# Batch norm after a matmul: the last chunk of the first column group in column layout, the row sums taken during it, and later normalisations on VectorE

## The chip, the cores and the metric

The kernel runs on one core of a Trainium2 chip. The metric is the device time of one execution in microseconds (us). Five engines work side by side, each on its own queue, in the order in which its instructions stand: TensorE (PE in the profile), VectorE (DVE), ScalarE (ACT), GpSimd (POOL) and SyncE (SP, which here only issues transfers). Sixteen DMA engines move the data between the memory of the chip and the core.

## The reference

```python
def reference(x, weight, gamma, beta, eps):      # x (16, 512, 1024), weight (1024, 768), f32
    y = np.matmul(x, weight)
    mean = np.mean(y, axis=(0, 1), keepdims=True)
    var = np.var(y, axis=(0, 1), keepdims=True)
    y_norm = (y - mean) / np.sqrt(var + eps)
    return (gamma * y_norm + beta).astype(np.float32)
```

So 8192 rows by 1024 are multiplied with 1024 by 768, and each of the 768 columns is normalised over all 8192 rows. No output of a column can be stored before all rows of that column are multiplied.

## The kernel before

**Tiling.** The rows are cut into C = 16 chunks of 512 (`CH`), a chunk into RT = 4 row tiles of 128. The columns are cut into NT = 6 column tiles of 128. The first GA = 3 column tiles are the first group (384 columns, half of the output); column tiles 3, 4 and 5 come after it, one at a time. x and the weight are read as f32 and cast to bf16 by the transfers that load them. GpSimd issues these (`load_x`, `load_w`); x is turned on VectorE (`turn_x`), so that the contraction lies on the partitions.

**Two layouts in the first group.** The chunks in `COLS` (line 58) are multiplied with the columns on the partitions (`mm`, line 184): 512 rows lie along the free dimension, VectorE takes the statistics of each column with `bn_stats` (`bn`, L297), ScalarE keeps the product in bf16 (`keep`, L300). Such a product must be transposed back by TensorE before it can be stored. The other ten chunks are multiplied with the rows on the partitions (`mm_rows`, L178). They need no transposing, but a column's sum then runs over the partitions: ScalarE squares the tile (`square`, L200), VectorE adds it to `sum1` (`add_rows`, L207), GpSimd adds the square to `sum2` (`add_squares`, L204; every fourth goes to VectorE and `sum3`), ScalarE keeps the tile in bf16 (`keep_rows`, L213). `merge_rows` (L216) adds `sum3` to `sum2`. Twelve small matmuls on TensorE (`sums_rows`, L234) add `sum1` and `sum2` over the partitions into the PSUM tile `tot`.

**The affine of the first group.** `part_cols` (L218) aggregates the statistics of the column chunks while row chunks are still being multiplied. `affine_rows` (L239) joins both parts to mean and variance, and makes scale and shift (the square root is on ScalarE, L247). For the column chunks these are used as they are. For the row chunks they must lie along the free dimension on every partition: two diagonal matrices times a matrix of ones (`spread_rows`, L264) put them there, and ScalarE copies the shift to `sum1` (L266).

**The outputs.** A row chunk is multiplied by the scale on VectorE (`norm_rows`, L272), shifted on GpSimd (`shift_rows`, L278), and stored in two pieces of 384 KB (`store_rows`, L282). A column chunk, and each chunk of column tiles 3 to 5, is normalised in place in bf16 (`norm`: on ScalarE in L317, on VectorE or GpSimd in L322), transposed on TensorE (`turn_y`, L338), copied from PSUM to the ring buffer on ScalarE (`out_copy`, L351), and stored (`store`, L356). Transposes that wait are taken up one after each matmul of `mm` (`turn_one`); the rest are flushed ahead of the copy. Tiles 3 and 4 give 8 blocks of 512 KB each, of two chunks. The last tile has its own plan (`last_outputs`), with buffers of its own (`o_sb`), since all that is left after the last product is its normalising, transposing, copying and storing.

**The order.** Nothing is decided while the kernel runs. Each step is put down with a due time, `at(t, function, ...)`; all are sorted by due time, and in that order they are appended to the queues of their engines. `pe` is the planned time of TensorE, `S` is `pe` at the end of the first group's products. `tk` is the due time of the column chunks' outputs and `tr` that of the row chunks'. Each engine keeps to its order: an instruction that waits holds all that stands behind it. The due times order the work and no more; the chip's times are in the profile. Input pieces and output pieces share one ring buffer (`piece`), eight PSUM banks serve all products and transposes, and all stores are issued by SyncE in one order.

Of the kernel before, what the change touches and what calls it, by code (L numbers as in the profile page):

```python
# [10 lines left out]
def kernel(  # L11
# [23 lines left out]
    nc = tc.nc  # L35
    f32 = mybir.dt.float32
    bf16 = mybir.dt.bfloat16
    AF = mybir.ActivationFunctionType
    ALU = mybir.AluOpType
# [5 lines left out]
    P = 128  # L45
# [3 lines left out]
    RT = CH // P  # L49
    C = M // CH  # L50
# [4 lines left out]
    EARLY = 5  # L55
    SHORT = 2
    GA = 3
    COLS = (0, 3, 5, 8, 10, 13)
    NA = GA * P
    GY = 3  # L60

# [3 lines left out]
    singles = ctx.enter_context(tc.tile_pool(name="singles", bufs=1))  # L65
# [7 lines left out]
    def seq(bi):  # L73

        ins = bi.ins
        prev = last.get(ins.engine)
        if prev is not None:
            tc.add_manual_dep(
                ins, prev,
                mybir.DependencyInfo(mybir.DependencyClass.NoSync, mybir.DependencyReason.DATA),  # L80
                reason="order",
            )
        last[ins.engine] = ins.name
        return bi
# [14 lines left out]
    sum2 = singles.tile([P, NA], f32)  # L99
    sum3 = singles.tile([P, NA], f32)  # L100
    for acc in (sum1, sum2, sum3):
        seq(nc.vector.memset(acc, 0.0))
    stats = singles.tile([P, NT, C, 6], f32)
    part1 = singles.tile([P, GA], f32)
    part2 = singles.tile([P, GA], f32)
    mv = singles.tile([P, NT, 2], f32)
    gamma_sb = singles.tile([P, NT], f32)
    beta_sb = singles.tile([P, NT], f32)
# [2 lines left out]
    tmp = singles.tile([P, NT], f32)  # L111
# [7 lines left out]
    xs, xT, py, ygrp, yrow, ops, ost, aff = {}, {}, {}, {}, {}, {}, {}, {}  # L119
# [4 lines left out]
    def piece(words):  # L124
        if head[0] + words > RING:
            head[0] = 0
        head[0] += words
        return ring[:, head[0] - words:head[0]]
# [71 lines left out]
        seq(nc.scalar.activation(sq_sb, py["row", c, s][:, 0:NA], AF.Square))  # L200

    def add_squares(c, s):
        eng, acc = (nc.vector, sum3) if s == RT - 1 and c < C - 2 else (nc.gpsimd, sum2)
        seq(eng.tensor_add(acc, acc, py.pop(("sq", c, s))))  # L204

    def add_rows(c, s):
# [7 lines left out]

    def merge_rows():
        seq(nc.gpsimd.tensor_add(sum2, sum2, sum3))  # L216

    def part_cols():  # L218

        g, share = slice(0, GA), len(COLS) / C  # L220
        for nt in range(GA):
            seq(nc.vector.bn_aggr(mv[:, nt, :], stats[:, nt, 0:len(COLS), :]))
        seq(nc.vector.tensor_mul(part2, mv[:, g, 0], mv[:, g, 0]))
        seq(nc.vector.tensor_add(part2, part2, mv[:, g, 1]))
        seq(nc.vector.tensor_scalar(part2, part2, share, None, op0=ALU.mult))
        seq(nc.vector.tensor_scalar(part1, mv[:, g, 0], share, None, op0=ALU.mult))

    def sums_rows():

# [9 lines left out]
    def affine_rows():  # L239
        g = slice(0, GA)  # L240
        mean, var = mv[:, g, 0], mv[:, g, 1]
        seq(nc.vector.tensor_add(mean, aff["tot"][:, 0:GA], part1))
        seq(nc.vector.tensor_mul(tmp[:, g], mean, mean))
        seq(nc.vector.tensor_sub(tmp[:, g], part2, tmp[:, g]))
        seq(nc.vector.tensor_add(var, aff["tot"][:, GA:2 * GA], tmp[:, g]))
        seq(nc.vector.tensor_scalar(var, var, 0.0, None, op0=ALU.max))
        seq(nc.scalar.activation(std[:, g], var, AF.Sqrt, bias=eps_sb, scale=1.0))  # L247
        seq(nc.vector.tensor_mul(tmp[:, g], mean, gamma_sb[:, g]))
        seq(nc.vector.reciprocal(std[:, g], std[:, g]))
        seq(nc.vector.tensor_mul(scale[:, g], std[:, g], gamma_sb[:, g]))  # L250
        diag = piece(2 * NA).rearrange("p (i a n) -> p i a n", i=2, n=P)
        aff["diag"] = diag
        for a in range(GA):
            seq(nc.vector.tensor_scalar(diag[:, 0, a], ident, scale[:, a:a + 1], None, op0=ALU.mult))
        seq(nc.vector.tensor_mul(tmp[:, g], tmp[:, g], std[:, g]))
        seq(nc.vector.tensor_sub(shift[:, g], beta_sb[:, g], tmp[:, g]))
        for a in range(GA):
            seq(nc.vector.tensor_scalar(diag[:, 1, a], ident, shift[:, a:a + 1], None, op0=ALU.mult))
# [36 lines left out]
    def bn(nt, c):  # L295
        i = c if nt >= GA else COLS.index(c)
        seq(nc.vector.bn_stats(stats[:, nt, i, :], py[nt, c]))  # L297
# [67 lines left out]
    def at(t, fn, *args):  # L365
        events.append((t, len(events), fn, args))
# [31 lines left out]
    pe = 0.0  # L398

    def rows_unit(c, s, jws=range(JW), span=ROW_US):  # L400
        nonlocal pe
        pe = max(pe, arrive[c * RT + s])
        at(pe, mm_rows, c, s, jws)
        pe += span
        if jws[-1] == JW - 1:
            at(pe + 0.2, square, c, s)
            at(pe + 0.7, add_rows, c, s)
            at(pe + 0.9, add_squares, c, s)
            at(pe + 1.6, keep_rows, c, s)

    def unit(nt, c, span, jws=range(JW)):
        nonlocal pe
        pe = max(pe, arrive[c * RT + RT - 1])
        at(pe, mm, nt, c, jws)
        pe += span
        if jws[-1] == JW - 1:
            at(pe + 0.2, bn, nt, c)
            at(pe + 1.0, keep, nt, c)
# [12 lines left out]
    pe = max(pe, arrive["w", 2])  # L431
    for nt in range(NT):
        unit(nt, 0, MM_US / 2, [2, 3])
    for c in range(1, C):
        if c in COLS:
            for nt in range(GA):
                unit(nt, c, MM_US)
        else:
            for s in range(RT):
                rows_unit(c, s)  # L440
        if c < EARLY:
            for nt in range(GA, NT):
                unit(nt, c, MM_US)
        if c == C - 2:
            at(pe + 0.5, part_cols)
            at(pe + 3.0, merge_rows)

    S = pe
    at(S + 2.0, sums_rows)
    at(S + 2.1, affine_rows)  # L450
    at(S + 5.5, spread_rows, 0)
    at(S + 5.6, spread_rows, 1)
    ga = tuple(range(GA))
    tr, tk = S + 7.2, S + 8.0
    for c in range(C):
        if c in COLS:
            for nt in range(GA):
                at(tk - 2.6 + 0.8 * nt, norm, nt, c, "act")
            for s in range(0, RT, 2):
                at(tk + 0.7 * s, turn_y, ga, c * CH + s * P, 2)  # L460
                at(tk + 0.7 * s + 1.9, out_copy, ga, c * CH + s * P, "act")
                at(tk + 0.7 * s + 2.7, store, ga, c * CH + s * P, 2)
            tk += 6.2
        else:
            for s in range(0, RT, 2):
                at(tr, norm_rows, c, s)
                at(tr + 1.1, shift_rows, c, s)
                at(tr + 3.0, store_rows, c, s)
                tr += 1.85

    def outputs(nt, t0, step):
        for b in range(C // 2):
            tb = t0 + step * b
            for i in range(2):
                at(tb - 1.4 + 0.5 * i, norm, nt, 2 * b + i, "act" if i or b < 2 else "dve")
            at(tb, turn_y, (nt,), 2 * b * CH, 2 * RT)
            at(tb + 2.2, out_copy, (nt,), 2 * b * CH, "act")
            at(tb + 2.3, store, (nt,), 2 * b * CH, 2 * RT)
# [16 lines left out]
    for nt in range(GA, NT):  # L495
        for c in range(EARLY, C):
            for jws in halves:
                unit(nt, c, MM_US / 2 + (0.12 if nt == GA else 0.17), jws)
        at(pe + 0.55, finish, nt)
        if nt == GA:  # L500
            outputs(nt, S + 40.0, 2.2)
        elif nt < NT - 1:
            outputs(nt, max(pe + 4.0, S + 55.0), 2.0)
        else:
            last_outputs(nt, pe + 3.0)
# [39 lines left out]
```

## Time and profile before

| what | before |
|---|---|
| time, median of 3 | 229.54 us (229.26 to 229.68) |
| span of the profiled execution | 228.0 us |
| TensorE busy | 202.1 us, 89% |
| VectorE busy | 149.0 us, 65% |
| ScalarE busy | 128.5 us, 56% |
| GpSimd busy | 122.7 us, 54% |
| read / written | 36.71 MB / 25.17 MB |
| loads, share of the 16 DMA engines | 59.1% |
| stores, share of the 16 DMA engines | 35.5% |

The span has three stages. To about 103 us x arrives, and the first group and part of the other tiles are multiplied as it comes. From there to 138 us nothing is transferred; the first group is finished at 125.97 us (the first product of the last stretch of `mm` starts there), its affine is done at 133.5. From 138 us to the end outputs are stored, while TensorE works through column tiles 3, 4 and 5, whose last statistics start at 202.7 us. After that only the last tile's outputs are left.

In the profile's rows an arrow reads "output from input", "x28" is a count, and brackets hold the idle time of the engine before an instruction with what ended it. An engine's share of the whole span says little here, since the three stages have different limits; stretches of the last stage say more.

### The profile page before, as it was taken

The numbers are of one execution on the slowest core, as the hardware profiler recorded it, in microseconds if no ns is written. First come the engines' busy times: TensorE is split into PE (matmuls) and PEld (weight loads), VectorE is DVE, ScalarE is ACT, GpSimd is POOL, SyncE is SP. The second block draws the span as 40 slices with busy tenths as digits, with TensorE's granted clock in tenths as the row PEclk, the third lists the DMA queues.
The fourth block names the chain that finished last, engine by engine and source line by source line (L and its number), as shares of the span: only waits on it lengthen the run. The fifth ranks groups of instructions, "written<-read, shape, count | busy, mean of one in ns | idle before, by whom it ended". The sixth has DMA issues, their size and how long they took to land. (4 is left out here: it accounts for less than half of the span.)

```text
span 228.0 us, 3342 instructions
## 1 busy us (share of the span) xinstructions
PE 202.1 (89%) x1148; PEld 104.6 (46%) x1166; DVE 149.0 (65%) x245; ACT 128.5 (56%) x224; POOL 122.7 (54%) x145
## 2 busy tenths in 40 slices
PE   7759999999999999999999999998999999876600
PEld 2333545444544654556456544444445555445400
DVE  3222888887787797978546387799786544348810
ACT  2001554442543664536546358788899999998300
POOL 8787595964765896615328409997998000002000
PEclk9988999999999999999999999999999999997755
DMA  5999999999999999980000004889896998998996
GB/s 63 166 187 186 174 196 196 197 194 196 192 192 196 197 196 196 196 116 0 0 0 4 0 0 175 293 303 337 320 358 235 314 294 236 263 282 248 285 283 207
DMA packets 70049, 43.74 MB, mean 192 GB/s; under 512 B 3984, under 2 KB 69520, under 8 KB 70032
## 3 DMA queue, kind: packets, MB, share of 16 engines
q0 software_dynamic: 34624, 18.36, 59.1%
q1 hardware_dynamic: 35408, 25.18, 35.5%
q8 instruction: 9, 0.15, 0.3%
q14 instruction: 8, 0.07, 0.1%
HBM read 36.71 MB, written 25.17 MB: 271 GB/s over the span
## 5 line engine op out<-in xcount | busy, mean ns | idle before, releaser
L188 PE MATMUL y_ps<-xT_sb,w_sb 128*128 128x512 bf16 (+1 forms) x522 | 130.7, 385 | 4.6 <-DVE xT_sb L166 2.1
L188 PEld LDWEIGHTS <-w_sb 128*128 128x128 bf16 x540 | 51.9, 97 | 69.1 <-issue 7.0
L300 ACT CAST y_sb<-y_ps 128x512 bf16<-128x512 f32 x66 | 39.8, 604 | 55.6 <-DVE stats L297 52.6
L297 DVE BATCH_NORM_STATS2 stats<-y_ps 128x6 f32<-128x512 f32 x66 | 44.8, 687 | 31.7 <-PE y_ps L188 30.9
L154 POOL DMA_DIRECT2D ring<-in_x_dram x72 | 45.3, 634 | 17.9 <-DVE xT_sb L166 9.6
L178 PE MATMUL y_ps<-w_sb,xT_sb 128*128 128x384 bf16 x320 | 53.1, 326 | 0.0
L338 PE MATMUL o_ps<-ident,y_sb 128*128 128x128 bf16 x264 | 45.4, 233 | 8.2 <-ACT y_sb L317 3.7
L166 DVE STREAM_TRANSPOSE xT_sb<-ring 128x1024 f32<-128x1024 f32 (+1 forms) x34 | 39.4, 1168 | 15.7 <-DMA ring<-in_x_dram 15.4
L204 POOL TENSOR_TENSOR sum<-sum,sq_sb 128x384 f32<-128x384 f32 x32 | 32.2, 1005 | 24.5 <-ACT sq_sb L200 23.5
L278 POOL TENSOR_TENSOR ring<-ring,sum 128x768 f32<-128x768 f32 x20 | 36.2, 1836 | 11.4 <-ACT sum L266 8.2
L178 PEld LDWEIGHTS <-xT_sb 128*128 128x128 bf16 x320 | 31.3, 98 | 21.6
L317 ACT ACTIVATE y_sb<-y_sb,shift,scale 128x512 bf16<-128x512 bf16 x38 | 31.5, 859 | 0.0
L351 ACT CAST ring<-o_ps 128x1024 f32<-128x1024 bf16 (+1 forms) x28 | 27.0, 988 | 5.3 <-POOL ring L278 2.1
L338 PEld LDWEIGHTS <-y_sb 128*128 128x128 bf16 x264 | 23.2, 103 | 14.0 <-ACT y_sb L317 6.7
L207 DVE TENSOR_TENSOR sum<-y_ps,sum 128x384 f32<-128x384 f32 x40 | 21.8, 545 | 11.3 <-ACT sq_sb L200 10.5
L200 ACT ACTIVATE sq_sb<-y_ps 128x384 f32<-128x384 f32 x40 | 19.5, 493 | 11.2 <-PE y_ps L178 9.7
L213 ACT CAST y_sb<-y_ps 128x384 bf16<-128x384 f32 x40 | 19.1, 477 | 7.2 <-DVE sum L207 7.1
L272 DVE TENSOR_TENSOR ring<-y_sb,a_ps 128x768 f32<-128x768 bf16 x20 | 18.6, 939 | 1.7 <-DMA out_dram<-ring 1.7
L322 POOL TENSOR_SCALAR y_sb<-y_sb,scale,shift 128x512 bf16<-128x512 bf16 x2 | 1.7, 845 | 30.2 <-DVE shift L311 30.2
L322 DVE TENSOR_SCALAR y_sb<-y_sb,scale,shift 128x512 bf16<-128x512 bf16 x26 | 11.6, 478 | 0.0
L147 PE MATMUL idle_ps<-idle_sb 128*128 128x512 bf16 x26 | 7.7, 468 | 1.2 <-DVE idle_sb L92 1.2
L141 POOL DMA_DIRECT2D w_sb<-in_weight_dram x12 | 6.1, 511 | 0.7 <-DMA ring<-in_x_dram 0.3
(49 smaller groups left out, 39.3 us busy)
## 6 DMA issues: line engine op xcount, KB each, us to landing
ring<-in_x_dram POOLq DMA_DIRECT2D x56, 256.0 KB, 9.1
out_dram<-ring SPq DMA_DIRECT2D x32, 384.0 KB, 3.1
out_dram<-ring SPq DMA_DIRECT2D x16, 512.0 KB, 4.0
out_dram<-o_sb SPq DMA_DIRECT2D x7, 512.0 KB, 6.5
ring<-in_x_dram POOLq DMA_DIRECT2D x16, 128.0 KB, 5.4
w_sb<-in_weight_dram POOLq DMA_DIRECT2D x8, 96.0 KB, 4.8
w_sb<-in_weight_dram POOLq DMA_DIRECT2D x4, 192.0 KB, 6.0
out_dram<-o_sb SPq DMA_DIRECT2D x2, 256.0 KB, 3.9
```

The costliest lines, as they stand in the source:

```text
L154: seq(nc.gpsimd.dma_start(x_bf[32 * i:32 * i + 32], src[:, :, KQ * i:KQ * (i + 1)]))
L166: seq(nc.vector.transpose(dst[:, half, :, jw0:jw1], src[:, :, jw0:jw1]))
L178: seq(nc.tensor.matmul(y_ps, xT[c][:, jw, s * P:(s + 1) * P, e], w_sb[:, jw, e, 0:NA], start=(jw == 0 and e == 0), stop=(jw == JW - 1 and ...
L188: seq(nc.tensor.matmul(y_ps, w_sb[:, jw, e, nt * P:(nt + 1) * P], xT[c][:, jw, q0 * QR:q1 * QR, e], start=(jw == 0 and e == 0 and q0 == 0) ...
L204: seq(eng.tensor_add(acc, acc, py.pop(("sq", c, s))))
L207: seq(nc.vector.tensor_add(sum1, py["row", c, s][:, 0:NA], sum1))
L278: seq(nc.gpsimd.tensor_add(o_sb, o_sb, sum1[:, None, :].to_broadcast([P, 2, NA])))
L297: seq(nc.vector.bn_stats(stats[:, nt, i, :], py[nt, c]))
L300: seq(nc.scalar.copy(y(nt, c), py.pop((nt, c))))
L317: seq(nc.scalar.activation(y(nt, c), y(nt, c), AF.Identity, bias=shift[:, nt:nt + 1], scale=scale[:, nt:nt + 1],))
L338: seq(nc.tensor.transpose(dst, src, ident))
L351: seq(nc.scalar.copy(o_sb, src))
```

## The change

Three things are done. The column chunks of the first group are spread evenly and the last chunk, 15, becomes one of them, so that the last row chunk is 14, and the sums over the partitions are taken between the second and the third unit of chunk 15. The aggregation of the column chunks then cannot be done early any more: it moves into `affine_rows`, which gets `bn_aggr` and a few small operations more, and `part_cols` goes. The outputs of the first group are due earlier, and the column chunks' more so than the row chunks'; chunk 0 is normalised on VectorE instead of ScalarE. And of column tiles 3 and 4 every normalisation that is due more than about 2 us after the last row chunk's outputs goes to VectorE, where before ScalarE took at least every second one. It is meant to let the outputs begin earlier, and to take work from ScalarE while outputs are stored.

```diff
-    COLS = (0, 3, 5, 8, 10, 13)
+    COLS = (0, 3, 6, 9, 12, 15)
...
     def add_squares(c, s):
-        eng, acc = (nc.vector, sum3) if s == RT - 1 and c < C - 2 else (nc.gpsimd, sum2)
+        eng, acc = (nc.vector, sum3) if s == RT - 1 and c < C - 3 else (nc.gpsimd, sum2)
...
-    def part_cols():
-
-        g, share = slice(0, GA), len(COLS) / C
-        for nt in range(GA):
-            seq(nc.vector.bn_aggr(mv[:, nt, :], stats[:, nt, 0:len(COLS), :]))
-        seq(nc.vector.tensor_mul(part2, mv[:, g, 0], mv[:, g, 0]))
-        seq(nc.vector.tensor_add(part2, part2, mv[:, g, 1]))
-        seq(nc.vector.tensor_scalar(part2, part2, share, None, op0=ALU.mult))
-        seq(nc.vector.tensor_scalar(part1, mv[:, g, 0], share, None, op0=ALU.mult))
...
     def affine_rows():
         g = slice(0, GA)
         mean, var = mv[:, g, 0], mv[:, g, 1]
-        seq(nc.vector.tensor_add(mean, aff["tot"][:, 0:GA], part1))
-        seq(nc.vector.tensor_mul(tmp[:, g], mean, mean))
-        seq(nc.vector.tensor_sub(tmp[:, g], part2, tmp[:, g]))
-        seq(nc.vector.tensor_add(var, aff["tot"][:, GA:2 * GA], tmp[:, g]))
+        share = len(COLS) / C
+        for nt in range(GA):
+            seq(nc.vector.bn_aggr(mv[:, nt, :], stats[:, nt, 0:len(COLS), :]))
+        seq(nc.vector.tensor_mul(msq, mean, mean))
+        seq(nc.vector.tensor_add(var, var, msq))
+        seq(nc.vector.scalar_tensor_tensor(
+            mean, mean, share, aff["tot"][:, 0:GA], op0=ALU.mult, op1=ALU.add))
+        seq(nc.vector.tensor_mul(msq, mean, mean))
+        seq(nc.vector.scalar_tensor_tensor(
+            var, var, share, aff["tot"][:, GA:2 * GA], op0=ALU.mult, op1=ALU.add))
+        seq(nc.vector.tensor_sub(var, var, msq))
         seq(nc.vector.tensor_scalar(var, var, 0.0, None, op0=ALU.max))
...
         if c in COLS:
             for nt in range(GA):
                 unit(nt, c, MM_US)
+                if c == C - 1 and nt == 1:
+                    at(pe, sums_rows)
...
-        if c == C - 2:
-            at(pe + 0.5, part_cols)
-            at(pe + 3.0, merge_rows)
+        if c == C - 3:
+            at(pe + 2.0, merge_rows)
 
     S = pe
-    at(S + 2.0, sums_rows)
-    at(S + 2.1, affine_rows)
-    at(S + 5.5, spread_rows, 0)
-    at(S + 5.6, spread_rows, 1)
+    at(S + 0.9, affine_rows)
+    at(S + 4.4, spread_rows, 0)
+    at(S + 4.5, spread_rows, 1)
     ga = tuple(range(GA))
-    tr, tk = S + 7.2, S + 8.0
+    tr, tk = S + 5.8, S + 5.0
     for c in range(C):
         if c in COLS:
             for nt in range(GA):
-                at(tk - 2.6 + 0.8 * nt, norm, nt, c, "act")
+                at(tk - (0.5 if c == 0 else 2.6 - 0.8 * nt), norm, nt, c, "dve" if c == 0 else "act")
...
-            tk += 6.2
+            tk += 6.2 if c else 5.0
...
-                at(tb - 1.4 + 0.5 * i, norm, nt, 2 * b + i, "act" if i or b < 2 else "dve")
+                at(tb - 1.4 + 0.5 * i, norm, nt, 2 * b + i, "act" if tb < tr + 2.0 else "dve")
```

More of the change, by code (lines that the diff above doesn't have):

```diff
@@ L103 @@
     stats = singles.tile([P, NT, C, 6], f32)
-    part1 = singles.tile([P, GA], f32)
-    part2 = singles.tile([P, GA], f32)
+    msq = singles.tile([P, GA], f32)
     mv = singles.tile([P, NT, 2], f32)
```

## The prediction

> **What bounds the kernel now.** I read the slices of the page first, then the stretches of the store stage, the waits, the chain of the end, and the timelines of single engines around the places that these pointed to.
>
> ```profile
> ACT  2001554442543664536546358788899999998300
> DMA  5999999999999999980000004889896998998996
> ...
> 170.00:180.00 10.00, 9.51 (x71) 5.24 (x73) 7.21 (x14) 10.00 (x17) 5.60 (x4) 1.00 0.80 275
> 180.00:190.00 10.00, 9.86 (x71) 5.20 (x70) 4.18 (x9) 10.00 (x15) 0.00 (x0) 1.00 1.00 297
> 190.00:200.00 10.00, 8.96 (x69) 5.00 (x69) 3.92 (x8) 10.00 (x15) 0.00 (x0) 1.00 0.85 243
> 200.00:205.00 5.00, 3.51 (x31) 2.06 (x30) 2.46 (x5) 5.00 (x8) 0.00 (x0) 1.00 0.99 280
> ```
>
> Input loads fill the DMA until about 103 us; TensorE then works off its backlog without stores; from 138 us the 25.2 MB of output are stored. In the stretches the busy columns are PE, PEld, DVE, ACT, POOL, then clock, DMA share, GB/s. From 170 to 205 us ScalarE is busy all the time, VectorE well under half of it after 180, GpSimd done. The DMA is nearly full, but not quite: 0.80 and 0.85.
>
> ```profile
> 194.91 0.23 PE L338 MATMUL o_ps<-ident,y_sb 128*128 128x128 bf16 x1 [0.97 <-ACT y_sb L317]
> 204.07 0.16 DVE L306 SCALAR_TENSOR_TENSOR tmp<-mv,gamma_sb 128x1 f32<-128x1 f32 x1
> 204.35 1.01 ACT L317 ACTIVATE y_sb<-y_sb,shift,scale 128x512 bf16<-128x512 bf16 x1
> 205.07 0.48 ACT L305 ACTIVATE std<-mv,eps_sb 128x1 f32<-128x1 f32 x1
> 205.72 2.14 ACT L351 CAST ring<-o_ps 128x1024 f32<-128x1024 bf16 x2
> 206.11 1.12 DVE y_sb L322 x2
> ```
>
> ScalarE runs late. TensorE stops for one of its normalisations (bracket: 0.97 us). The last column tile's variance is there at 204.03, but its square root starts only at 205.07, behind a normalisation; the normalisations of that tile start at 206.11, and two output copies of the tile before it still follow at 205.72.
>
> ```profile
> L356 SPq DMA_DIRECT2D out_dram<-o_sb x9: 626/1413/2002, 209.3 to 220.3; - x9
> 206.00:208.00 2.00, 1.33 (x12) 1.07 (x12) 1.96 (x5) 2.00 (x4) 1.68 (x2) 0.63 0.77 227
> 212.00:214.00 2.00, 1.19 (x14) 1.00 (x15) 2.00 (x6) 0.80 (x1) 0.00 (x0) 0.84 0.97 287
> 224.00:226.00 2.00, 0.00 (x0) 0.00 (x0) 0.00 (x0) 0.00 (x0) 0.00 (x0) 0.50 0.92 290
> 226.00:228.00 2.00, 0.00 (x0) 0.00 (x0) 0.00 (x0) 0.00 (x0) 0.00 (x0) 0.50 0.20 60
> ```
>
> The nine stores of the last tile are 7 x 512 KB + 2 x 256 KB = 4.19 MB. At the 285 GB/s of these stretches that is 14.7 us, and the last data moves at 226.4, 1.6 us before the end. So the end is: start of pure tail + 14.7 + 1.6; here the tail starts at about 211.7. Two things can set that start: the last tile being ready, and the DMA having worked off all older stores. The older ones are 12.58 MB in rows of 1536 bytes at about 366 GB/s (34.4 us) and 8.39 MB in rows of 512 bytes at 283 (29.6 us): 64 us. They begin to move at 139.3. By two-microsecond stretches the DMA's shortfall from 140 to 208 adds up to 7.9 us: 3.6 before 162, 2.1 in 172 to 178, 1.4 in 190 to 196, 0.7 in 204 to 208. 139.3 + 64 + 7.9 = 211.2, within 0.5 of the start found.
>
> [...]
>
> ```profile
> 174.61 1.54 DVE L322 TENSOR_SCALAR y_sb<-y_sb,scale,shift 128x512 bf16<-128x512 bf16 x1
> 179.58 0.40 DVE L322 TENSOR_SCALAR y_sb<-y_sb,scale,shift 128x512 bf16<-128x512 bf16 x1
> ```
>
> The first ran while GpSimd still added, the second after. [...]
>
> **Part 1, chunk positions.** TensorE's work is the same: six column chunks and ten row chunks stay, with as many transposes. One more row chunk falls ahead of 100 us (4, 5, 7, 8, 10, 11 for 4, 6, 7, 9, 11): on VectorE 5 adds of 0.55 against 3 statistics of 0.69, +0.7 us; on GpSimd 3 adds of 1.0. This lies beside TensorE, which is four chunks (some 16 us) behind the last arrival at 103 us. I take 0; bound 0 to 0.3.
>
> **Part 2, the row sums.** The last square of the last row chunk comes one chunk (5.3 us) earlier, so GpSimd's adds, that ended at 128.30, end near 123, and the twelve sum matmuls (1.25 us) find them done at about 124.3. They stand ahead of the last column unit, so that group ends at 127.25 instead of 125.97. Then on VectorE, in one chain: the last statistics 127.45, +0.61; three aggregations 0.66 (as at L222); six small operations 0.2 each. The maximum is over near 130.0, against 131.06: 1.0 us gained. The scalar_tensor_tensor forms I price at 0.2 by L311 (0.21); bound 0.16 to 0.64, the mean at L306, where one of three met GpSimd, which is idle here. Queued behind this chain on VectorE are the statistics of two units of column tile 3; they were held until 133.47 before, 132.4 now.
>
> ```profile
> 136.00 0.47 ACT L266 COPY sum<-a_ps 128x384 f32<-128x384 f32 x1
> 136.54 3.61 POOL L278 TENSOR_TENSOR ring<-ring,sum 128x768 f32<-128x768 f32 x2 [8.23 <-ACT sum L266]
> 138.39 0.40 SPq L282 DMA_DIRECT2D out_dram<-ring  x1
> ```
>
> These are the old start of the outputs. The new one: spread matmuls 131.75 to 133.65, three normalisations of chunk 0 on VectorE done by 134.7, GpSimd from about 135.5 (-1.0). Chunk 0's transposes are planned at S+5.0 for S+8.0, so its six transposes, copy and store come out near 136.7, ahead of the first row store. Stores begin to move about 0.9 us after the issue, as before (138.39 to 139.3): 137.7, a gain of **1.6 us** for the DMA. TensorE may wait some 0.4 us for chunk 0's normalisations, as it does now (0.34 at 138.42): 0.
>
> **Part 3, the engine of the normalisations.** By the code, ScalarE had 10 of 16 normalisations in each of column tiles 3 and 4; now 6 and 0, and chunk 0's three go too: 17 x 0.72 = 12.2 us less on ScalarE between 135 and 205. VectorE takes 17 x 0.40 = 6.8 us, where after 180 it idles about 1.24 us in each unit of 2.25 waiting for TensorE: hidden, and nothing waits behind them. GpSimd's adds end near 174.9, the first moved normalisation that could meet them is due about 175: 0 taken, bound 1.2 us for one meeting.
>
> In the steady part ScalarE needs, per unit of TensorE (2.25 us), 0.72 + 0.46 + 0.91 = 2.09 us with one normalisation, so its backlog from 170 hardly shrinks; without it 1.37, so the backlog is gone. The last square root starts when the variance is there: 1.0 us gained. TensorE's work from 125.97 to the last product is 33 units x 1.8 + 1.25 + 1.9 + 192 transposes x 0.056 = 73.3 us, so 199.3 against 202.7: 3.4 us of waits, of which 0.34, 0.51, 0.97 are marked as ScalarE's. I take 1.5 us as gone; bound 0.5 to 2.5.
>
> **Sum.** Ready: the first copy of the last tile ended at 208.2 (its store was held to 209.3 by older stores); 208.2 - 1.0 - 1.5 + 0.1 + 0.9 = 206.7. DMA free: 137.7 + 64 + remaining shortfall. The 1.4 and the 0.7 late ones go with ScalarE's backlog, some of the 2.1 may: 5.3 left gives 207.0. Tail from 207.0: + 14.7 + 1.6 = 223.3 span. The measured median is 1.54 above the profiled span: 224.8; with 0.2 for part 1's bound, **225.0 us**.
>
> **Rivals.** (B) The transfers keep their gaps: the earlier start only moves work from one hole to another, because TensorE's pace hands out the blocks. Then 137.7 + 64 + 7.9 = 209.6, + 16.3 + 1.54 = **227.4**. For it: the DMA is at 0.99 in 196 to 204, so little can be compressed there; against: the gaps at 190 to 196 stand beside the ScalarE wait. (C) VectorE becomes the late one: moved normalisations meet GpSimd's adds at 1.54 each, or row statistics fall behind in the load stage. Four meetings are 4.6 us on VectorE; its idle time covers some 2 of these, TensorE waits for the rest and gives nothing back: 229.54 + 2.6 - 1.0 for the square root = **231.1**. Against: the due times put them past GpSimd's end. (D) The tail is bound by something that I have not seen and nothing moves: 229.5.
>
> **Chances.** My forecast 0.62 (224 to 226.2, by TensorE's 0.5 to 2.5 and a shortfall of 4 to 6.5), B 0.27 (226.2 to 228.6), C 0.08, D 0.03. Faster 0.89, same 0.03, slower 0.08. Range 223.3 to 228.1: below lies the case of all waits gone, above C, D and the end of B.
>
> **What would show it.** After the change: ScalarE below 8 of 10 from 180 on; the last square root within 0.1 us of its variance; last statistics near 201; first store near 136.8; no VectorE normalisation at 1.5 us; DMA share over 0.95 from 178 to the end and a tail of 4.19 MB that starts near 207. It is wrong if TensorE shows new waits on VectorE's normalisations or on banks, if the DMA has a hole at 172 to 178 larger than 2.1 us, or if the last statistics stay at 202.7.

## The result, and the profile after

The changed kernel takes **223.52 us** (median of 4, 222.68 to 223.81) against 229.43 us before. The ratio is 0.9736, with a 95% interval of 0.9707 to 0.9765. The forecast of 225.0 us has the right side and the right size; the median lies 1.5 us below it and 0.2 us above the lower end of the range. The profiled execution, the fastest of the four, has a span of 220.9 us.

Busy tenths in 40 slices, then the stretches of the store stage, in the same columns as before (PE, PEld, DVE, ACT, POOL, clock, DMA share, GB/s):

```profile
ACT  2001553533554556465466217878889976868310
DMA  5999999999999999990000002999889999998997
```

```profile
170.00:180.00 10.00, 10.00 (x74) 5.30 (x72) 6.53 (x16) 9.46 (x15) 3.43 (x2) 1.00 1.00 325
180.00:190.00 10.00, 10.00 (x78) 5.58 (x77) 6.64 (x16) 6.87 (x9) 0.00 (x0) 1.00 0.91 258
190.00:200.00 10.00, 9.62 (x77) 5.42 (x76) 6.12 (x15) 7.07 (x10) 0.00 (x0) 1.00 0.96 278
200.00:205.00 5.00, 2.83 (x28) 2.04 (x28) 4.49 (x11) 3.99 (x7) 1.68 (x2) 0.80 0.87 244
```

ScalarE is down from 10.00 to 6.87 and 7.07, VectorE up from 4.18 and 3.92 to 6.64 and 6.12, and TensorE is busy without a gap from 170 to 198. The DMA share is 0.91, 0.96 and 0.87 from 180 to 205 us, so one of the signs that the prediction named, over 0.95 from 178 to the end, is not met. The timelines of single engines at the two ends of the stage:

```profile
135.86 0.40 SPq L352 DMA_DIRECT2D out_dram<-ring  x1
...
174.32 0.40 DVE L318 TENSOR_SCALAR y_sb<-y_sb,scale,shift 128x512 bf16<-128x512 bf16 x1
...
198.89 0.70 DVE L293 BATCH_NORM_STATS2 stats<-y_ps 128x6 f32<-128x512 f32 x1 [0.92 <-PE y_ps L187]
...
200.43 0.29 ACT L301 ACTIVATE std<-mv,eps_sb 128x1 f32<-128x1 f32 x1 [0.43 <-DVE mv L300]
201.09 1.93 ACT L347 CAST ring<-o_ps 128x1024 f32<-128x1024 bf16 x2
```

The first store is issued at 135.86 instead of 138.39. The first VectorE normalisation of column tile 3 takes 0.40 us; GpSimd's last add was over at 173.4. The last statistics begin at 198.89 instead of 202.71. The bracket of the square root has turned round: ScalarE is there and waits 0.43 us for the aggregation. Still, the last two copies of column tile 4 come behind it, at 201.09.

The tail holds the surprise. The stores of the last tile, and two stretches, one inside column tile 4's stores, one inside the last tile's:

```profile
L352 SPq DMA_DIRECT2D out_dram<-o_sb x9: 530/1228/2208, 203.5 to 214.3; - x9
```

```profile
192.00:194.00 2.00, 2.00 (x17) 1.09 (x16) 1.34 (x3) 1.50 (x2) 0.00 (x0) 1.00 0.98 281
214.00:216.00 2.00, 0.00 (x0) 0.00 (x0) 0.00 (x0) 0.00 (x0) 0.00 (x0) 0.50 1.15 347
```

Both move rows of 512 bytes. Column tile 4's go at 281 GB/s, as before. The last tile's go at 347, where they went at 285 before, in the same nine stores. The prediction had nothing that could do this. (The DMA share is 1.15 there, over 1, so it can't be read as a share of a fixed limit.)

### The profile page after: what moved, and what is told of

Same layout as the page of the kernel before. It is cut to its first block, busy times and chain, and to the rows that moved or that the text cites. A ratio compares the mean times of both kernels' runs of the same rounds, so it can differ in the third digit from the quotient of the medians.

```text
span 220.9 us, 3354 instructions
## 1 busy us (share of the span) xinstructions
PE 201.6 (91%) x1166; PEld 104.7 (47%) x1166; DVE 151.1 (68%) x260; ACT 117.5 (53%) x207; POOL 122.4 (55%) x145
## 4 chain that ended last, share of the span: by engine, by line
PE 83%; DMA 5%; DVE 4%; POOL 3%; issue 1%; ACT 0%; POOLq 0%
PE y_ps L187 52%; PE y_ps L177 24%; PE o_ps L334 7%; DMA w_sb<-in_weight_dram 3%; DMA ring<-in_x_dram 2%; DVE o_sb L349 2%; POOL w_sb L140 2%; POOL ring L153 1%; DVE y_sb L318 1%; PE a_ps L260 1%; PE tot_ps L223 1%; DVE stats L293 0%; DVE mv L300 0%; ACT std L301 0%; DVE rstd L305 0%
## 5 line engine op out<-in xcount | busy, mean ns | idle before, releaser
L296 ACT CAST y_sb<-y_ps 128x512 bf16<-128x512 f32 x66 | 38.6, 585 | 52.0 <-DVE stats L293 49.1
L334 PE MATMUL o_ps<-ident,y_sb 128*128 128x128 bf16 x264 | 46.4, 236 | 4.6 <-DVE y_sb L318 4.4
L347 ACT CAST ring<-o_ps 128x1024 f32<-128x1024 bf16 (+1 forms) x28 | 25.8, 924 | 12.6 <-ACT y_sb L296 5.8
L334 PEld LDWEIGHTS <-y_sb 128*128 128x128 bf16 x264 | 24.1, 106 | 9.1 <-DVE y_sb L318 5.8
L313 ACT ACTIVATE y_sb<-y_sb,shift,scale 128x512 bf16<-128x512 bf16 x21 | 16.3, 814 | 0.0
L318 DVE TENSOR_SCALAR y_sb<-y_sb,scale,shift 128x512 bf16<-128x512 bf16 x43 | 16.1, 423 | 0.0
```

Source lines behind the costliest of these rows:

```text
L296: seq(nc.scalar.copy(y(nt, c), py.pop((nt, c))))
L318: seq((nc.vector if eng == "dve" else nc.gpsimd).tensor_scalar(y(nt, c), y(nt, c), scale[:, nt:nt + 1], shift[:, nt:nt + 1], op0=ALU.mult, ...
L334: seq(nc.tensor.transpose(dst, src, ident))
L347: seq(nc.scalar.copy(o_sb, src))
```

## The experiments

Each diff is against the kernel that its text names. A name such as e5_before_aligned in an expectation counts the experiments in the order in which they stand here. Ratios, with their 95% intervals, are to the kernel before, run alongside each time (medians of 229.0 to 229.5 us). Where a kernel is called slower than the changed one, the two intervals touch in some cases, but the single runs do not: they are 222.68 to 223.81 us for the changed kernel, and 224.16 or more for those.

**The engine rule alone** (kernel before):

```diff
-                at(tb - 1.4 + 0.5 * i, norm, nt, 2 * b + i, "act" if i or b < 2 else "dve")
+                at(tb - 1.4 + 0.5 * i, norm, nt, 2 * b + i, "act" if tb < tr + 2.0 else "dve")
```

> The kernel before with one line of the change alone: the normalisations of column tiles 3 and 4 that are due after the last row chunk's outputs go to VectorE (14 fewer on ScalarE). Theory A, ScalarE's backlog is the larger part (TensorE's waits of up to 3.4 us, and 1.0 us at the last square root): last statistics near 200, square root at once, 225 us. Theory B, the earlier first store is what counts, since the DMA is the limit of the store stage: 228 us, with the last statistics earlier but the tail held up by older stores. In both the first store stays at 138.4.

Measured: 227.93 us, ratio 0.9934 (0.9913 to 0.9955). That is theory B's number. The two lines show what theory A had wrong (timelines of TensorE and VectorE):

```profile
177.23 0.23 PE L338 MATMUL o_ps<-ident,y_sb 128*128 128x128 bf16 x1 [1.11 <-ACT y_sb L317]
```

```profile
202.35 0.70 DVE L297 BATCH_NORM_STATS2 stats<-y_ps 128x6 f32<-128x512 f32 x1 [0.92 <-PE y_ps L188]
```

The square root did follow its variance at once (203.89), but the last statistics moved by only 0.36 us. TensorE meets ScalarE's backlog at 177.23, 1.11 us, where it used to meet it at 194.91. That the first group's column chunks build it up, before the moved normalisations begin, is tested further down. Theory B's account isn't what is seen either: it had the last statistics earlier and the tail held up. What changed is a gap of the DMA at 190 to 196 us, which closed; one stretch of it, in the kernel before and in this one:

```profile
192.00:194.00 2.00, 1.87 (x16) 0.95 (x14) 1.01 (x2) 2.00 (x4) 0.00 (x0) 1.00 0.62 185
192.00:194.00 2.00, 2.00 (x19) 1.13 (x17) 0.87 (x2) 1.90 (x3) 0.00 (x0) 1.00 0.99 286
```

Added up by two-microsecond stretches, as in the prediction, the DMA's shortfall fell from 7.9 to 6.3 us, about as much as the time did (1.4 us).

**The engine rule undone** (changed kernel, the same line turned back):

> The changed kernel with the old rule for the engine in column tiles 3 and 4 (ScalarE takes 20 of 32 normalisations again), all else as changed. Theory A: the early start alone gives little, ScalarE is at 10 of 10 again from about 170 us, the last square root waits, 227.5 us. Theory B: most of the gain stays, 225 us. The first store stays at 135.9 in both.

Measured: 225.38 us, 0.9812 (0.9756 to 0.9867), so the rule is worth 1.9 us in the changed kernel. ScalarE is at 10.00 of 10 again from 180 to 200 us, the square root starts at 202.75, 1.1 us after its variance (201.67), and the last statistics begin at 200.35. ScalarE's timeline:

```profile
202.75 0.43 ACT L301 ACTIVATE std<-mv,eps_sb 128x1 f32<-128x1 f32 x1
```

Of TensorE's marked waits for ScalarE ahead of the last products only one is left, 0.65 us at 192.55. The time is between the theories' numbers, nearer to B: a large part of the gain survives without the rule. Here, too, the tail ran at 347 GB/s, and in the first experiment at 285, which a difference in ScalarE's load can't explain.

**Only the last blocks** (kernel before):

```diff
-                at(tb - 1.4 + 0.5 * i, norm, nt, 2 * b + i, "act" if i or b < 2 else "dve")
+                at(tb - 1.4 + 0.5 * i, norm, nt, 2 * b + i, "dve" if nt > GA and b >= 5 else "act" if i or b < 2 else "dve")
```

> The kernel before with only the last three blocks of column tile 4 normalised on VectorE (3 normalisations off ScalarE, 2.2 us). It takes ScalarE's delay at the last square root (1.0 us) and at the copies behind it away, and leaves TensorE's waits before 195 us as they are. Theory A1, the delay at the end is what ScalarE's backlog costs: square root at once, 227.5 us or less. Theory A2, TensorE's waits are what it costs: at most 0.5 us gained, 229.0 us.

Measured: 228.93 us, 0.9961 (0.9937 to 0.9985), theory A2. The square root came at once (204.37, 0.43 us of waiting for the aggregation), and the last tile's first store was issued at 207.48 instead of 209.3, yet only 0.4 us came of it by the medians (0.9 by the ratio). That is about the gap which the DMA had at 204 to 208 us (0.7 us) and has no more; its share is now 0.97 or more from there to 216 us. It was still busy with older stores, and the rest of being ready earlier is hidden.

**Meeting GpSimd** (changed kernel):

```diff
-                at(tb - 1.4 + 0.5 * i, norm, nt, 2 * b + i, "act" if tb < tr + 2.0 else "dve")
+                at(tb - 1.4 + 0.5 * i, norm, nt, 2 * b + i, "act" if tb < tr - 8.0 else "dve")
```

> The changed kernel with the rule moved 10 us earlier, so that all 16 normalisations of column tile 3 are on VectorE; the first ones are due while GpSimd still adds. [...] three or four normalisations take 1.5 us or more instead of 0.40, statistics queued behind them come late, TensorE waits, and the time is 0.5 to 2 us over the changed kernel (224 to 225.5 us). If not, 0.40 us each and no difference (223.5 us).

Measured: 225.12 us, 0.9806 (0.9752 to 0.9861), 1.6 us over the changed kernel. VectorE's timeline:

```profile
166.40 1.57 DVE L318 TENSOR_SCALAR y_sb<-y_sb,scale,shift 128x512 bf16<-128x512 bf16 x1
...
169.34 2.30 DVE L318 TENSOR_SCALAR y_sb<-y_sb,scale,shift 128x512 bf16<-128x512 bf16 x2
...
176.12 0.39 DVE L318 TENSOR_SCALAR y_sb<-y_sb,scale,shift 128x512 bf16<-128x512 bf16 x1
```

Beside GpSimd's adds, whose last ends at 175.12, single normalisations take up to 1.57 us, after them 0.39. TensorE waited three times for VectorE's normalisations (0.23, 0.49, 0.54 us), and the last statistics came at 200.43. The changed kernel moves only what is due after the last row chunk's outputs, which GpSimd adds to; this is what that limit is worth.

**Where the buffers lie.** What differed in the tail was found in the allocation, not in the order of work. In the kernel before, two scratch tiles of 12 bytes start at bytes 61600 and 61632 of a partition and the next tile at 61664, so each takes 32 bytes. The change has three lines that the diff above leaves out:

```diff
-    part1 = singles.tile([P, GA], f32)
-    part2 = singles.tile([P, GA], f32)
+    msq = singles.tile([P, GA], f32)
```

They replace these two tiles by one, and so everything allocated behind them lies 32 bytes lower. The last tile's output buffers all started 32 bytes over a multiple of 256 before, the lowest at byte 61984 of a partition; after, they all start at multiples of 256, the lowest at 61952 = 242 x 256. The ring buffer, allocated ahead of them, starts at 16512 in both, 128 over a multiple of 256. Four kernels test it. The first changes nothing but this in the kernel before:

```diff
-    part1 = singles.tile([P, GA], f32)
-    part2 = singles.tile([P, GA], f32)
+    parts = singles.tile([P, 2, GA], f32)
+    part1, part2 = parts[:, 0], parts[:, 1]
```

> The kernel before with its two 12-byte scratch tiles made one (each takes 32 bytes), so that all buffers allocated behind them lie 32 bytes lower: those of the last tile's stores start at 61952 = 242 x 256 bytes in a partition, as in the changed kernel, instead of at 61984. Instructions and their order are the same. Theory P (position): the last tile's stores run at 347 GB/s as in the changed kernel, not at 285, which is 4.19 MB in 12.1 us instead of 14.7: 2.2 us faster, 227.2 us. Theory Q (the different rate comes from the order or timing of stores, or from the execution): 229.4 us, 285 GB/s.

The second takes it away from the changed kernel:

```diff
     warm = singles.tile([P, 1], f32)
+    spare = singles.tile([P, 8], f32)
+    seq(nc.vector.memset(spare, 0.0))
```

> The changed kernel with one unused 32-byte tile (and one memset at the start), so that the buffers of the last tile's stores start at 61984 again. Theory P: they run at 285 GB/s, 2.2 us slower than the changed kernel, 225.7 us, which is within 1 us of my forecast of 225.0. Theory Q: 223.5 us, 347 GB/s.

Measured: 227.20 us for the first, 0.9911 (0.9878 to 0.9944); 225.21 us for the second, 0.9814 (0.9782 to 0.9846). Both are near theory P's numbers, and on its side. The same stretch of the tail, in the first and in the second:

```profile
214.00:216.00 2.00, 1.24 (x14) 0.88 (x12) 2.00 (x5) 0.81 (x1) 0.00 (x0) 0.50 1.15 347
```

```profile
214.00:216.00 2.00, 0.00 (x0) 0.00 (x0) 0.00 (x0) 0.00 (x0) 0.00 (x0) 0.50 0.95 281
```

The kernel before, with its instructions unchanged, has the tail of the changed one; the changed kernel, shifted, has the tail of the one before. The position is worth 2.3 us in the first and 1.7 us in the second. In the last tile's stores the kernel before, the changed one and the first eleven experiments fall in line: the full stretches show 346 to 348 GB/s in the nine kernels whose buffers start at multiples of 256, and 275 to 295 in the other four.

**The ring buffer moved to a multiple of 256** (changed kernel; four of the small tiles go ahead of the ring, so it starts at 16640 and the total stays; the tiles in between, the weights among them, move up by 128 bytes too):

```diff
+    gamma_sb = singles.tile([P, NT], f32)
+    beta_sb = singles.tile([P, NT], f32)
+    std = singles.tile([P, NT], f32)
+    scale = singles.tile([P, NT], f32)
     ring = singles.tile([P, RING], f32)
```

> The changed kernel with four 32-byte tiles allocated ahead of the ring buffer instead of behind it: the ring starts at 16640 = 65 x 256 bytes instead of 16512, nothing else moves. Theory P: the 512-byte rows of tiles 3 and 4 go from 283 to 347 GB/s, the 1536-byte rows from 366 to 390 or more [...]. TensorE and the readiness of the last tile stay, so the end moves little: the tail no longer begins behind older stores, 222.5 us. If the DMA were still what sets the end: 218 us. Theory Q: 223.5 us.

Measured: 223.18 us, 0.9715 (0.9681 to 0.9749): 0.3 us under the changed kernel, and the two intervals overlap. But the rates moved as theory P has it. The 1536-byte rows in the changed kernel, then in this one, then the 512-byte rows of column tile 4 in this one:

```profile
164.00:166.00 2.00, 1.96 (x15) 0.93 (x13) 1.37 (x3) 1.27 (x3) 2.00 (x2) 1.00 1.01 363
```

```profile
164.00:166.00 2.00, 1.95 (x14) 0.83 (x12) 1.36 (x3) 1.54 (x3) 2.00 (x2) 1.00 1.07 400
190.00:192.00 2.00, 2.00 (x19) 1.21 (x18) 1.33 (x3) 2.00 (x4) 0.00 (x0) 1.00 1.15 346
```

363 became 400 GB/s, 281 became 346. (The loads into the same ring show no difference: 196 GB/s from 40 to 60 us in both kernels.) The end hardly moved, it seems, because the DMA now waits for blocks: it moves 217 to 228 GB/s at 182 to 190 and 196 to 202 us, and TensorE hands out one block of 512 KB in a unit of 2.25 us (the statistics of two units start at 194.85 and 197.10), which is an estimate of 233 GB/s. Besides, the last two blocks of column tile 4 are still copied behind the square root (201.56 here), and their stores stand ahead of the last tile's.

**Output blocks due earlier as well** (the kernel just shown):

```diff
-            outputs(nt, S + 40.0, 2.2)
+            outputs(nt, S + 40.0, 1.73)
...
-            outputs(nt, max(pe + 4.0, S + 55.0), 2.0)
+            outputs(nt, max(pe + 4.0, S + 53.84), 1.73)
```

> As e7_ring_aligned, and the 16 output blocks of tiles 3 and 4 are due every 1.73 us instead of every 2.2 and 2.0, so that the last two blocks (1.05 MB) are copied and stored ahead of the last square root instead of behind it. The last tile's stores then find an empty DMA: first store near 203, 0.9 us to the first data, 12.1 us of data, 1.6 us to the end: span 218, 219.6 us. Against it: 16 more transposes ahead of the last products (0.9 us on TensorE). If the older stores were not in the way: as e7_ring_aligned.

Measured: **220.70 us**, 0.9622 (0.9593 to 0.9650), faster than both kernels, 2.8 us under the changed one. ScalarE and SyncE:

```profile
199.21 1.03 ACT L347 CAST ring<-o_ps 128x1024 f32<-128x1024 bf16 x1
200.20 0.29 ACT L301 ACTIVATE std<-mv,eps_sb 128x1 f32<-128x1 f32 x1
...
201.96 1.29 ACT L347 CAST o_sb<-o_ps 128x512 f32<-128x512 bf16 x2 [0.99 <-PE o_ps L334]
```

```profile
200.27 0.37 SPq L352 DMA_DIRECT2D out_dram<-ring  x1
202.57 10.56 SPq L352 DMA_DIRECT2D out_dram<-o_sb  x9
```

The last copy of column tile 4 is now ahead of the square root, its store at 200.27, and the last tile's stores find the way free at 202.57. The same due times without the moved ring were not run, so the 2.5 us between this kernel and the one before it belong to the pair.

**Old due times** (changed kernel with the first group's affine, spread and outputs due as before):

> The changed kernel with the due times of the first group's affine and outputs as before (and chunk 0 on ScalarE again); chunk positions, early sums and the new rule for the engine stay. Theory S1, the early due times are what the early start is worth: first store back near 138, last statistics near 202, 225.5 us. Theory S2, the earlier sums by themselves bring it, since the affine runs as soon as they are there: 224 us or less.

**Only the column chunks late** (changed kernel; `tk` from S+8.0 in steps of 6.2, chunk 0 on ScalarE):

> The changed kernel with the due times of the column chunks' outputs alone as before (first at S+8.0 instead of S+5.0, chunk 0 on ScalarE); the row chunks' stay early. Theory S3, ScalarE's share is what matters: the column chunks' normalisations and copies are the part of the early start that takes ScalarE's backlog away, and without it TensorE waits again: 225.2 us, near e9_old_due_times. Theory S4, the first row store's time matters: 223.8 us.

Measured: 224.90 us, 0.9801 (0.9756 to 0.9846), for the first, and 225.27 us, 0.9815 (0.9771 to 0.9858), for the second. In the first the first store is at 136.71 and the last statistics at 200.71, which lies between the theories. In the second the row chunks start early (first store at 136.50) and it gains nothing: the column chunks' due times are the part that counts, theory S3. (The mirror, column chunks early and row chunks late, was not run.) TensorE's timeline in the second:

```profile
176.11 0.23 PE L334 MATMUL o_ps<-ident,y_sb 128*128 128x128 bf16 x1 [1.11 <-ACT y_sb L313]
```

This is the wait of the first experiment, with the same 1.11 us: column outputs that end late push ScalarE's normalisations of column tile 3 back. Early column outputs take it away.

**The tail without GpSimd** (the 220.70 us kernel; chunks 2 and 3 of the last tile on VectorE):

```diff
-        blocks = [((0,), "v", "act"), ((1,), "v", "act"), ((2, 3), "gg", "dve"), ((4, 5), "vv", "act")]
+        blocks = [((0,), "v", "act"), ((1,), "v", "act"), ((2, 3), "vv", "dve"), ((4, 5), "vv", "act")]
```

> As e8_ring_aligned_outputs_early, with chunks 2 and 3 of the last tile normalised on VectorE instead of GpSimd. There four VectorE normalisations took 2.21 us beside GpSimd's two (0.40 each without them, 0.31 apart). Six in a row should take some 2.0 us and the third store come about 0.5 us earlier: 220.3 us. If the DMA's stretch after 204 hides it: 220.7 us.

Measured: 221.14 us, 0.9637 (0.9587 to 0.9688), not told apart from 220.70. Six normalisations took 2.02 us, as estimated, but the copy for the third store began 2.92 us after the square root (204.00 after 201.08) where it had begun 3.09 us after it (203.29 after 200.20): 0.17 us instead of 0.5. Nothing is gained here.

**Position and engine rule together** (kernel before):

> The kernel before with the buffers 32 bytes lower (as e5_before_aligned) and the new rule for the engine (as e1_engine_only); chunk positions, sums and due times as before. If the parts add up: 227.2 - 1.5 = 225.7 us, and what lies between this and e9_old_due_times (224.9) is the worth of chunk positions and early sums alone, 0.8 us. If the older stores hide the shorter tail once ScalarE is relieved: 226.5 us or more. If the engine rule is worth more with the shorter tail: 225 us or less, and the early sums alone nothing.

Measured: 226.25 us, 0.9860 (0.9810 to 0.9911), between the first two expectations: the parts add up to within 0.6 us. From here to the kernel with the old due times (224.90) lie chunk positions and early sums, some 1.3 us; the two intervals overlap, the single runs (225.75 to 226.87 and 224.61 to 225.46) do not.

## Why the prediction was right, and where its terms were off

**The whole.** With the buffers where the prediction, unknowing, took them to be, the changed kernel takes 225.21 us, against 225.0 forecast. The remaining 1.7 us to 223.52 is the position of the buffers. The step that failed is "Tail from 207.0: + 14.7 + 1.6": the tail was priced at the old 285 GB/s, and 4.19 MB at 347 are 12.1 us. The diff showed the cause, two small tiles less and one more, and I costed those lines at nothing without a word. By these rates the term is 2.6 us too long, and in the profiled executions the last data does move 2.6 us earlier (218.9, against 221.5 in the shifted kernel); the medians show 1.7. Single executions of one kernel differ by up to 1.1 us here, and where the other 0.9 us lies stays open.

**Part 1**, chunk positions: taken as 0, bound 0.3. TensorE shows no wait of 0.1 us or more between 95 us and the last products in the changed kernel. Nothing speaks against it, but the positions were not run alone.

**Part 2**, the row sums: the maximum was put near 130.0 and ends at 129.33; the first group ended half a microsecond before my reckoning. (Executions of one order scatter by as much at this point: the kernel before and three of its variants reach it between 125.97 and 126.64.) The scalar_tensor_tensor forms took 0.15 us each, under the price of 0.2. The first store was put near 136.7 and came at 135.86, so the DMA gained 2.5 us instead of 1.6.

**Part 3**, the engine: ScalarE's load and the square root came as forecast, VectorE's moved normalisations met no add (0.40 to 0.41 us each from 174 to 199 us), and TensorE did not wait for them. (A normalisation on ScalarE takes 0.80 to 0.82 us in the kernel before until 175 us, with a mean of 0.81, and the next instruction starts 0.72 us after it, as at 135.28 and 136.00; after 175 us the mean is 0.92 and the longest takes 1.01. Why is not shown.) The size of TensorE's gain was off: 3.8 us at the last statistics, where I took 1.5 with an upper bound of 2.5. Half a microsecond of it was there at the end of the first group, which is no more than the scatter just named. What can be compared is the time from that end to the last statistics. In the kernel before it includes the twelve sum matmuls (1.25 us); where they come ahead of the group's last unit they are added. In the changed kernel the sums start at 123.67, and the last unit (1.8 us) runs from 124.93 to 126.7 (timeline of TensorE):

```profile
123.67 1.39 PE L223 MATMUL tot_ps<-ones,sum 128*128 128x1 f32 x12
124.93 6.51 PE L187 MATMUL y_ps<-xT_sb,w_sb 128*128 128x512 bf16 x28
```

| kernel | from the first group's end to the last statistics, sums included |
|---|---|
| before | 76.7 us |
| engine rule alone | 76.2 us |
| with the rule, chunk positions and early sums (old due times) | 75.2 us |
| row chunks due early too (only the column chunks late) | 75.1 us |
| changed | 73.4 us |

Each is one profiled execution, but others with the same order of work agree to 0.1 us (two more at 76.7, two at 73.4). In this order the rule brings 0.6 us, positions and sums 1.0, the column chunks' early outputs 1.8. The prediction's 73.3 us for TensorE's work is met, so nearly all of the 3.4 us that it called waits went, and not 1.5. And the cause was put in the wrong place. I gave TensorE's waits to the normalisations of column tiles 3 and 4; but with the rule alone, and with the old due times, three marked waits for ScalarE are left, together 1.96 and 1.95 us (1.82 before). They go only when the column chunks of the first group are output early as well, since that is what keeps ScalarE from falling behind by 175 us. My part 2 priced the early column outputs by their first store alone.

**Why 3.8 us on TensorE did not show.** "DMA free" was put at 207.0. Three stretches of the shifted kernel, as the stores begin, in column tile 4 and at the end:

```profile
136.00:138.00 2.00, 2.00 (x13) 0.96 (x12) 1.81 (x3) 2.00 (x4) 2.00 (x2) 1.00 0.60 212
188.00:190.00 2.00, 2.00 (x22) 1.23 (x19) 0.86 (x3) 1.67 (x3) 0.00 (x0) 1.00 0.80 231
220.00:222.00 2.00, 0.00 (x0) 0.00 (x0) 0.00 (x0) 0.00 (x0) 0.00 (x0) 0.50 0.71 224
```

The last stretch with data has a share of 0.71 where full ones have 0.95, so the last data moves at about 221.5; less 14.7 that is 206.8. The last tile's first store was issued at 203.5 already. So the older stores, not the last tile, set the start of the tail, as in the sum's larger term, and TensorE's extra was hidden. The shortfall of the DMA between 138 and 204 us, by two-microsecond stretches, is 5.6 us against 5.3 estimated. The sum again with what was measured: data from 136.8 instead of 137.7, + 64 + 5.6 = 206.4. Of the two terms that were too small, TensorE's was hidden, and the start of the stores was partly spent on the larger shortfall.

That the shortfall came out near the estimate is in part luck. The sum kept some 1.7 us of the gap at 172 to 178 us and let the late gaps go with ScalarE's backlog. In the shifted kernel it is the other way: nothing is left at 172 to 178, and there are new late gaps, 1.1 us at 184 to 190 and 0.9 at 198 to 204. In them the DMA moves 228 to 261 GB/s, often near the 233 at which TensorE hands out blocks.

**Rivals.** B, that the gaps of the DMA stay (227.4), was wrong in its number: the shortfall fell from 7.9 to 5.6 us. Its reason, that TensorE's pace hands out the blocks, fits the late gaps that are left; that is read from the rates and not tested. The engine rule alone comes near B's number (227.93) by another way, with the old start of the stores and one gap less. C, VectorE as the late one, needs the meeting with GpSimd; forced, it costs 1.6 us over the changed kernel, and the due times avoid it. D said that something unseen binds the tail. There was such a thing, the position of the buffers, but it moved with the change, where D had it that nothing moves.

## What to carry to other kernels

Read an engine's backlog where it builds up, not only where it shows: here TensorE's wait at 195 us only moved to 177 when ScalarE's later work was taken away, and went when the work due from 140 on was moved as well. When the last transfers set the end, ask for each gain whether the last piece is ready earlier or only waits longer behind older stores; the way free and the piece ready must move together, as in the 220.70 us kernel. And look at the start address of every buffer that is stored in short rows: here a tiny tile more or less in front of it was worth 2.3 us of 229.5 in one kernel and 1.7 us of 223.5 in the other.

## What the hardware did that I had not expected

Stores of 512-byte rows ran at about 285 GB/s from buffers that start 32 or 128 bytes over a multiple of 256, and at 346 to 348 from buffers at a multiple of 256; a multiple of 512 (61952, 347 GB/s) was no better than one of 256 alone (16640, 346 GB/s). Rows of 1536 bytes went from 363 to 400. The ratio of the rates of the two rows, 283/366 = 0.77 in the kernel before, is 346/400 = 0.87 from buffers at a multiple of 256. The 512-byte rows gain as much from either offset, a factor of 1.22 (347/285 from 32 over, 346/283 from 128 over). Why the start address acts on the rate is not shown, and other offsets were not tried.
